# A table's loads pinned in the load queue, and their wait for sixteen writes

## The chip, the core and the metric

The kernel runs on one core of a Trainium2 chip. The core has five engines that follow their own in-order queues: PE (TensorE, matrix products), DVE (VectorE), ACT (ScalarE), POOL (GpSimd) and SP (SyncE, which here issues loads). The metric is the device time of one execution in microseconds (us); lower is better. Runs of this kernel agree within about 0.06%, so that a difference of 0.2% can be told from none.

## What is computed

Two transformer blocks follow one another on 256 tokens of width 2048. The change touches only the last part of the second block, a layer of 16,384 small experts. Its reference, cut down:

```
q = (hb @ w_query).reshape(PEER_BLOCK, PEER_HEADS, 2, D_KEY // 2)
s = einsum('thpc,hpnc->thpn', q, sub_keys)      # scores against 2 x 128 keys, 8 heads
...                                             # top 16 pairs per head and token: idx, best_s
g = softmax(best_s)
u_sel = take(u, idx);  a = gelu(einsum('thkd,td->thk', u_sel, hb))
v_sel = take(v, idx)
out = einsum('thk,thkd->td', g * a, v_sel)
```

The kernel gathers no rows of `u` and `v`. It computes the activations of all 16,384 experts for all tokens (the first product, with `u`), multiplies them by a table of gates that is zero wherever a token did not choose an expert, and multiplies the result by all of `v` (the second product). The table lies in the chip's memory: `gd`, one value for each pair of expert and token.

## The kernel before

**The first product** is driven in `experts_in` by `linear`, over 128 column tiles `c` of 128 experts. Its weights `in_pu` come in 256 loads of 512 KB (`half`, line 289, tile `raw`, four buffers). Each is split in two parts by ACT (line 276, `whi`, a rounded copy) and DVE (line 261, `wlo`, the rest), in two pieces of 128x512 each, so that three matrix products in fast format (`ph`·`whi`, `pl`·`whi`, `ph`·`wlo`, into the accumulator `plin`) give the accuracy of one in full format. `expert` ends each column tile: DVE scales the accumulator into `et` (line 261), ACT applies GELU and writes it to `A` (line 273).

**The table** is filled beside the first product. `choose` (DVE) finds experts `EI` and gates `GT`; `scatter` then has POOL issue 256 indirect writes with accumulation (line 1660), 128 for each half of the tokens, one slot for 128 tokens at a time. Sixteen writes belong to one head, so there are sixteen groups of sixteen. Two pairs of one head are never equal, but pairs of different heads can be, so each group waits until all sixteen writes before it have landed.

**The second product** is `experts_out`. For each of 128 steps `j` a tile `g` of the table (128x256, 128 KB) is loaded by SP (line 1766), POOL multiplies it by `A` (line 258), and ACT and DVE split the product into `wh` and `wl` (lines 276 and 261). Two weight loads of `in_pv` follow, split the same way, and 24 matrix products per load into eight accumulators `o`. At the end DVE adds the residual `res`, and the result is stored.

**The order of the work.** A scheduler sets each engine's order when the program is built, from a simulated timeline of its own. Code under `tc.high_priority()` may be moved ahead of code that stands before it: the weight loads and splits in `half`, and the load, product and split of `g` in `experts_out`. An engine runs its queue strictly in that order, so an instruction that waits holds up all that is queued behind it. `keep_in_program_order` takes an instruction out of that freedom; `add_manual_dep` adds an edge: `Sync` makes a wait, `NoSync` only an order on one engine.

Of the kernel before, what the change touches and what calls it, by code (L numbers as in the profile page):

```python
# [8 lines left out]
F32 = mybir.dt.float32  # L9
# [8 lines left out]
S = 256  # L18
# [226 lines left out]
class Kernel:  # L245
# [1339 lines left out]
    def experts_in(self):  # L1585

        nc = self.nc
        es = ExitStack()
        sp = self.sp = self.pool("sp", 1, es)
        ap = self.pool("ap", 1, es)  # L1590
        rf = self.rf
        self.iota = self.ones
        nc.sync.dma_start(self.iota, self.io["iota"])

        self.EI = [sp.tile([128, 128], U32, name=f"EI{b}") for b in range(2)]
        self.GT = [sp.tile([128, 128], F32, name=f"GT{b}") for b in range(2)]
        t = sp.tile([128, 128], F32, name="dg")
        self.tokc = sp.tile([128, 2], F32, name="tokc")
        self.vtt(t, self.ident, self.iota, OP.mult)
        nc.vector.tensor_reduce(self.tokc[:, 0:1], t, axis=AX.X, op=OP.add)  # L1600
        self.ts(self.tokc[:, 1:2], self.tokc[:, 0:1], 128.0, None, OP.add)
        self.chosen = set()

        def slot(name):
            return ap.tile([128, 32, S], F32, name=name, tag="A", bufs=4)

        s1, s2, s3 = (slot(n).rearrange("p c t -> p (c t)") for n in ("s1", "s2", "s3"))
        qx = s1[:, 0:4096].rearrange("p (c t) -> p c t", t=S)
        scv = s1[:, 4096:8192].rearrange("p (b c n) -> p b c n", b=2, n=NKEY)
        keys = s2[:, 0:2048].rearrange("p (c n) -> p c n", n=NKEY)  # L1610
        nc.sync.dma_start(keys, self.io["keys"])
        pq = {}

        def query(c, p):
            self.vtt(qx[:, c], p, rf, OP.mult)
            if c % 4 == 0:
                pq[0], pq[1] = self.ps("psc"), self.ps("psc")
            for tb in range(2):
                self.mm(pq[tb][:, 128 * (c % 4):128 * (c % 4) + 128], qx[:, c, 128 * tb:128 * tb + 128], keys[:, c])
                if c % 4 == 3:  # L1620
                    self.acp(scv[:, tb, c - 3:c + 1], pq[tb].rearrange("p (c n) -> p c n", c=4))

        self.lin(self.io["w_pq"], 0, KT, KT, self.pxh, self.pxl, S, query)
        A = self.A = {}

        def expert(c, p):
            k, i = divmod(c, 32)
            if k not in A:
                A[k] = slot(f"A{k}")
            t = sp.tile([128, S], F32, name="et", tag="et", bufs=3)  # L1630
            self.vtt(t, p, rf, OP.mult)
            self.act(A[k][:, i], t, AF.Gelu)

        self.drive(self.linear(self.io["pu"], 0, NKEY, KT, self.pxh, self.pxl, S, expert),
                   [[self.both(self.choose(0, scv[:, 0], s2[:, 2048:4096], s2[:, 4096:8192]),
                               self.choose(1, scv[:, 1], s3[:, 2048:4096], s3[:, 4096:8192]))],
                    [self.scatter()]], EVERY3, (1,))
        self.rstack.close()
        return es
# [110 lines left out]
    def experts_out(self, es):  # L1750
        nc, A, sp = self.nc, self.A, self.sp
        with ExitStack() as c:
            vp = self.pool("vp", 2, c)
            op = self.pool("op", 1, c)
            acc = self.pool("acc", 1, c, space=PSUM)

            P = [[None] * 4 for _ in range(2)]
            for d in (3, 2, 0, 1):
                for b in range(2):
                    P[b][d] = acc.tile([128, 512], F32, name=f"o{b}{d}")  # L1760
            table = self.gd.rearrange("(i j t) o -> i j (t o)", j=NKEY, t=S)
            for j in range(NKEY):
                w = A[j // 32][:, j % 32]
                with self.tc.high_priority():
                    g = sp.tile([128, S], F32, name="g", tag="g", bufs=2)
                    nc.sync.dma_start(g, table[:, j])
                    self.gtt(g, w, g, OP.mult)
                    wh, wl = ((sp if j == 0 else vp).tile([128, S], F32R, name=n) for n in ("wh", "wl"))
                    self.split(wh, wl, g)
                for hf in range(2):  # L1770
                    hi, lo = self.half(self.io["pv"][2 * j + hf])
                    first, last = j == 0, j == NKEY - 1
                    for d in range(2):
                        for b in range(2):
                            ts = slice(128 * b, 128 * b + 128)
                            for l, r, st, en in ((wh, hi, first, False), (wh, lo, False, False), (wl, hi, False, last)):
                                self.mm(P[b][2 * hf + d], l[:, ts], self.block(r, 4 * d, 4), st, en)
            res = op.tile([128, 2, D], F32, name="res")
            nc.sync.dma_start(res, self.hd.rearrange("b p d -> p b d"))
            for b in range(2):  # L1780
                for d in range(4):
                    r = res[:, b, 512 * d:512 * d + 512]
                    self.vtt(r, P[b][d], r, OP.add)
                    nc.sync.dma_start(self.out[128 * b:128 * b + 128, 512 * d:512 * d + 512], r)
        es.close()
# [20 lines left out]
```

## Time and profile before

| | us |
|---|---|
| median of three runs | 3704.99 |
| the three runs | 3704.28 to 3706.61 |
| the profiled execution | 3704.27 |
| its span in the trace | 3702.5 |

The trace divides the span into busy time of each engine. PE is busy for 93% of it and bounds the kernel in almost every stage. The exception is one stretch, two slices of 40 long, in which PE, DVE and ACT are all idle and only POOL works. The span leaves out 1.77 us of the profiled execution's time.

### The profile page before, as it was taken

The numbers are of one execution on the slowest core, as the hardware profiler recorded it, in microseconds if no ns is written. First come the engines' busy times: TensorE is split into PE (matmuls) and PEld (weight loads), VectorE is DVE, ScalarE is ACT, GpSimd is POOL, SyncE is SP. The second block draws the span as 40 slices with busy tenths as digits, with TensorE's granted clock in tenths as the row PEclk, the third lists the DMA queues.
The fourth block names the chain that finished last, engine by engine and source line by source line (L and its number), as shares of the span: only waits on it lengthen the run. The fifth ranks groups of instructions, "written<-read, shape, count | busy, mean of one in ns | idle before, by whom it ended". The sixth has DMA issues, their size and how long they took to land.

```text
span 3702.5 us, 72372 instructions
## 1 busy us (share of the span) xinstructions
PE 3449.7 (93%) x28376; PEld 3238.5 (87%) x28376; DVE 2289.7 (62%) x4248; ACT 1764.2 (48%) x3187; POOL 869.4 (23%) x788
## 2 busy tenths in 40 slices
PE   8999999999999999999999999996019999999999
PEld 7899899999999999999999999996019988888887
DVE  6677777755555576565675998553005556666565
ACT  5444555545454554444554555552005555555554
POOL 2222221300000043000120006777760011111111
PEclk9999999999999999999999999998559999999999
DMA  5334545667676755443466567775225577666666
GB/s 196 110 111 136 162 145 155 202 196 218 196 221 194 221 189 164 143 148 120 132 188 195 184 187 186 186 188 103 0 32 185 187 226 211 212 211 212 212 211 195
DMA packets 230279, 635.99 MB, mean 172 GB/s; under 512 B 58320, under 2 KB 75408, under 8 KB 229552
## 3 DMA queue, kind: packets, MB, share of 16 engines
q1 hardware_dynamic: 193072, 631.22, 54.8%
q0 software_dynamic: 36864, 0.15, 2.5%
q8 instruction: 222, 3.64, 0.4%
q14 instruction: 121, 0.99, 0.1%
HBM read 610.16 MB, written 21.10 MB: 170 GB/s over the span
## 4 chain that ended last, share of the span: by engine, by line
PE 89%; POOL 5%; DVE 2%; issue 2%; DMA 2%; ACT 0%; SPq 0%; DVEq 0%; POOLq 0%; ACTq 0%
PE plin L255 63%; PE o L255 19%; POOL gd L1660 5%; DMA gd<-GT,EI 1%; PE po L255 1%; DVE wlo L261 1%; PE pfz L255 1%; PE pw L255 0%; DMA hd<-ht 0%; PE pz L255 0%; PE pbc L255 0%; PE pix L255 0%; PE pcs L255 0%; PE px L751 0%; PE pt L751 0%
## 5 line engine op out<-in xcount | busy, mean ns | idle before, releaser
L261 DVE TENSOR_TENSOR wlo<-raw,whi 128x512 fp32r<-128x512 f32 x2208 | 1615.4, 733 | 974.6 <-ACT whi L276 919.2
L276 ACT ACTIVATE whi<-raw 128x512 fp32r<-128x512 f32 x2208 | 1389.2, 630 | 1438.6 <-PE plin L255 1004.5
L255 PE MATMUL plin<-ph,whi 128*128 128x256 f32 (+1 forms) x4560 | 1285.7, 282 | 212.1 <-ACT whi L276 210.5
L255 PE MATMUL plin<-ph,wlo 128*128 128x256 f32 (+1 forms) x4560 | 1290.4, 283 | 2.2 <-DVE wlo L261 2.2
L255 PE MATMUL plin<-pl,whi 128*128 128x256 f32 (+1 forms) x4560 | 1290.4, 283 | 0.0
L255 PEld LDWEIGHTS plin<-ph,whi 128*128 128x128 f32 x4560 | 863.1, 189 | 213.8 <-ACT whi L276 210.7
L255 PEld LDWEIGHTS plin<-ph,wlo 128*128 128x128 f32 x4560 | 863.4, 189 | 4.7 <-DVE wlo L261 2.6
L255 PEld LDWEIGHTS plin<-pl,whi 128*128 128x128 f32 x4560 | 858.2, 188 | 1.6 <-issue 1.1
L1660 POOL DMA_INDIRECT gd<-GT,EI x256 | 407.1, 1590 | 415.4 <-DVE wlo L261 296.6
L255 PE MATMUL o<-whi,wl 128*128 128x512 f32 x1024 | 405.5, 396 | 0.0
L255 PE MATMUL o<-wlo,wh 128*128 128x512 f32 x1024 | 404.5, 395 | 0.0
L255 PE MATMUL plin<-xh,whi 128*128 128x256 f32 x1136 | 329.3, 290 | 9.1 <-ACT whi L276 8.1
L255 PE MATMUL plin<-xh,wlo 128*128 128x256 f32 x1136 | 328.9, 290 | 4.1 <-DVE wlo L261 3.9
L255 PE MATMUL plin<-xl,whi 128*128 128x256 f32 x1136 | 328.2, 289 | 1.5 <-DVE xl L264 1.5
L255 PE MATMUL o<-whi,wh 128*128 128x512 f32 x1024 | 321.9, 396 | 0.6 <-ACT whi L276 0.6
L258 POOL TENSOR_TENSOR g<-A,g 128x256 f32<-128x256 f32 x128 | 103.3, 808 | 816.2 <-DMA g<-gd 786.5
L255 PE MATMUL plin<-uh,wlo 128*128 128x256 f32 x1024 | 289.7, 283 | 0.0
L255 PE MATMUL plin<-ul,whi 128*128 128x256 f32 x1024 | 289.7, 283 | 0.0
L255 PE MATMUL plin<-uh,whi 128*128 128x256 f32 x1024 | 289.6, 283 | 0.0
L255 PEld LDWEIGHTS o<-whi,wh 128*128 128x128 f32 x1024 | 192.3, 188 | 47.3 <-issue 0.7
L255 PEld LDWEIGHTS o<-whi,wl 128*128 128x128 f32 x1024 | 192.2, 188 | 47.3
L255 PEld LDWEIGHTS plin<-xh,whi 128*128 128x128 f32 x1136 | 220.9, 195 | 13.8 <-ACT whi L276 9.4
(563 smaller groups left out, 3462.8 us busy)
## 6 DMA issues: line engine op xcount, KB each, us to landing
raw<-in_pu_dram SPq DMA_DIRECT2D x256, 512.0 KB, 3.7
raw<-in_pv_dram SPq DMA_DIRECT2D x256, 512.0 KB, 4.3
raw<-in_w_in_dram SPq DMA_DIRECT2D x208, 512.0 KB, 3.5
raw<-in_w_up_dram SPq DMA_DIRECT2D x128, 512.0 KB, 4.5
raw<-in_w_down_dram SPq DMA_DIRECT2D x128, 512.0 KB, 4.1
raw<-in_w_mix_dram SPq DMA_DIRECT2D x32, 512.0 KB, 3.6
gd<-zero SPq DMA_DIRECT2D x64, 256.0 KB, 5.2
raw<-in_w_out_dram SPq DMA_DIRECT2D x32, 512.0 KB, 3.6
```

The lines of the kernel that those rows point to most:

```text
L255: self.nc.tensor.matmul(out, l, r, start=start, stop=stop)
L258: self.nc.gpsimd.tensor_tensor(out, a, b, op=op)
L261: return self.nc.vector.tensor_tensor(out, a, b, op=op)
L276: return self.nc.scalar.activation(out, a, AF.Copy, **kw)
L1660: i = self.nc.gpsimd.indirect_dma_start(self.gd, bass.IndirectOffsetOnAxis(self.EI[tb][:, s:s + 1], 0), self.GT[tb][:, s:s + 1], None, com ...
```

## The change

Three lines change in kind. The ring of `et` goes from three buffers to two; the ring of `g` goes from two to three. Every load of `g` is kept in program order, so that it stands in SP's queue behind the loads that the code issues before it, all of `in_pu` among them. The first load of `g` gets a wait for each of the last sixteen writes (`self.scattered`), and every later one an order edge to the one before it.

```
-            t = sp.tile([128, S], F32, name="et", tag="et", bufs=3)
+            t = sp.tile([128, S], F32, name="et", tag="et", bufs=2)
...
+            sync, order = (mybir.DependencyInfo(c, mybir.DependencyReason.DATA)
+                           for c in (mybir.DependencyClass.Sync, mybir.DependencyClass.NoSync))
+            prev = None
             for j in range(NKEY):
                 w = A[j // 32][:, j % 32]
                 with self.tc.high_priority():
-                    g = sp.tile([128, S], F32, name="g", tag="g", bufs=2)
-                    nc.sync.dma_start(g, table[:, j])
+                    g = sp.tile([128, S], F32, name="g", tag="g", bufs=3)
+                    i = self.tc.keep_in_program_order(nc.sync.dma_start(g, table[:, j]))
+
+                    for x in [prev] if prev else self.scattered:
+                        self.tc.add_manual_dep(i.ins, x.ins.name, order if prev else sync, reason="the table is complete")
+                    prev = i
```

SP's queue before, where the first load of the table stands (`raw` is a weight load, `g` a tile of the table; the numbers are buffers):

```order
L289 DMA raw_33783<-in_pu_dram 128x1024
L289 DMA raw_33818<-in_pu_dram 128x1024
L1766 DMA g_36607<-gd_9608 128x256
L1766 DMA g_36658<-gd_9608 128x256
L289 DMA raw_33857<-in_pu_dram 128x1024
L1766 DMA g_36709<-gd_9608 128x256
L289 DMA raw_33892<-in_pu_dram 128x1024
```

And SP's queue with the change, at the place where these loads now stand:

```order
L289 DMA raw_36614<-in_pv_dram 128x1024
L289 DMA raw_36636<-in_pv_dram 128x1024
L289 DMA raw_36665<-in_pv_dram 128x1024
L289 DMA raw_36687<-in_pv_dram 128x1024
L289 DMA raw_36716<-in_pv_dram 128x1024
L1769 DMA g_36607<-gd_9608 128x256
L1769 DMA g_36658<-gd_9608 128x256
L1769 DMA g_36709<-gd_9608 128x256
L289 DMA raw_36738<-in_pv_dram 128x1024
L1786 DMA res_43135<-hd_25560 128x2x2048
```

The three first table loads have moved past the rest of the first product's weights and past five loads of the second's.

ACT's queue before, around the split of the table's first tile, `wh_36610` (`whi` are parts of weights, `A2` a column tile of activations):

```order
L276 ACTIVATE whi_33711<-raw_33709 128x512
L276 ACTIVATE whi_33715<-raw_33709 128x512
L276 ACTIVATE whi_33746<-raw_33744 128x512
L276 ACTIVATE wh_36610<-g_36607 128x256
L276 ACTIVATE whi_33750<-raw_33744 128x512
L273 ACTIVATE A2_31854<-et_33705 128x256
L276 ACTIVATE whi_33785<-raw_33783 128x512
```

ACT's queue with the change, around the same split:

```order
L273 ACTIVATE A3_34223<-et_36444 128x256
L276 ACTIVATE whi_36616<-raw_36614 128x512
L276 ACTIVATE whi_36620<-raw_36614 128x512
L276 ACTIVATE whi_36638<-raw_36636 128x512
L276 ACTIVATE whi_36642<-raw_36636 128x512
L273 ACTIVATE A3_34223<-et_36518 128x256
L276 ACTIVATE wh_36610<-g_36607 128x256
L276 ACTIVATE wh_36661<-g_36658 128x256
L276 ACTIVATE wh_36712<-g_36709 128x256
L276 ACTIVATE whi_36667<-raw_36665 128x512
```

The split has moved from among the first product's weights to behind its last GELU (`et_36518`) and behind the splits of the second product's first two weight loads. DVE's half of the split moves with it.

## Rows read from the trace of the kernel before

**Rows 1.** The page: span, engines' busy time, and busy tenths in 40 slices.
```profile
span 3702.5 us, 72372 instructions
...
PE 3449.7 (93%) x28376; PEld 3238.5 (87%) x28376; DVE 2289.7 (62%) x4248; ACT 1764.2 (48%) x3187; POOL 869.4 (23%) x788
...
PE   8999999999999999999999999996019999999999
...
POOL 2222221300000043000120006777760011111111
PEclk9999999999999999999999999998559999999999
```
**Rows 2.** Waits, 2540 to 2800 us: who waited for whom, us, times, longest.
```profile
ACT wh L276 <- POOL g L258: 214.3, 1, 214.3
...
PE plin L255 <- ACT whi L276: 210.5, 1, 210.5
...
POOL gd L1660 <- DMA gd<-GT,EI: 17.2, 7, 4.2
```
**Rows 3.** Timeline: start, duration, engine, line, operation, [idle before].
```profile
2759.66 1.54 POOL L1660 DMA_INDIRECT gd<-GT,EI  x1 [0.30 <-issue]
2762.64 0.80 SPq L1766 DMA_DIRECT2D g<-gd  x2
...
2764.92 1.40 POOL L258 TENSOR_TENSOR g<-A,g 128x256 f32<-128x256 f32 x2 [3.72 <-DMA g<-gd]
2765.68 0.42 ACT L276 ACTIVATE wh<-g 128x256 fp32r<-128x256 f32 x1 [214.34 <-POOL g L258]
```
**Rows 4.** Timeline of PE at both ends of the wait and between the products.
```profile
2555.85 0.28 PE L255 MATMUL plin<-ph,wlo 128*128 128x256 f32 x1
2766.66 0.58 PE L255 MATMUL plin<-ph,whi 128*128 128x256 f32 x1 [210.54 <-ACT whi L276]
...
2980.01 0.28 PE L255 MATMUL plin<-ph,wlo 128*128 128x256 f32 x1
...
2980.85 0.48 PE L255 MATMUL o<-whi,wh 128*128 128x512 f32 x1 [0.56 <-ACT whi L276]
```
**Rows 5.** Windows: length, busy us of PE, PEld, DVE, ACT, POOL, PE clock, DMA.
```profile
2232.00:2556.00 324.00, 324.00 (x2740) 323.92 (x2738) 207.24 (x365) 166.03 (x285) 244.69 (x151) 1.00 0.76 184
2556.00:2558.00 2.00, 0.12 (x2) 0.00 (x0) 0.00 (x0) 0.00 (x0) 1.70 (x2) 1.00 0.21 0
2558.00:2560.00 2.00, 0.00 (x0) 0.00 (x0) 0.00 (x0) 0.00 (x0) 1.64 (x2) 0.67 0.21 0
2560.00:2766.00 206.00, 0.00 (x0) 0.00 (x0) 0.00 (x0) 0.33 (x2) 159.78 (x105) 0.50 0.21 3
2766.66:2770.00 3.34, 3.33 (x14) 3.11 (x15) 2.64 (x5) 2.10 (x5) 1.17 (x1) 0.50 0.61 162
2770.00:2771.00 1.00, 1.00 (x9) 1.00 (x9) 0.97 (x2) 0.77 (x2) 0.00 (x0) 0.84 0.99 320
...
3000.00:3690.00 690.00, 690.00 (x2958) 555.46 (x2958) 422.60 (x616) 349.60 (x616) 98.45 (x122) 1.00 0.69 210
```
**Rows 6.** Timeline of POOL: the first writes of five groups of sixteen.
```profile
2265.85 1.92 POOL L1660 DMA_INDIRECT gd<-GT,EI  x1 [2.96 <-DMA gd<-GT,EI]
...
2305.10 1.54 POOL L1660 DMA_INDIRECT gd<-GT,EI  x1 [5.01 <-DMA gd<-GT,EI]
...
2339.59 2.02 POOL L1660 DMA_INDIRECT gd<-GT,EI  x1 [4.71 <-DMA gd<-GT,EI]
...
2543.59 1.54 POOL L1660 DMA_INDIRECT gd<-GT,EI  x1 [4.23 <-DMA gd<-GT,EI]
...
2731.98 1.55 POOL L1660 DMA_INDIRECT gd<-GT,EI  x1 [2.20 <-DMA gd<-GT,EI]
```
**Rows 7.** POOL's writes in two stretches, 2339 to 2543.5 and 2543.5 to 2762.
```profile
L1660 POOL DMA_INDIRECT gd<-GT,EI x96 | 152.9, 1593 | 51.5 <-issue 27.8 <-DMA gd<-GT,EI 20.1 <-DVE wlo L261 3.7
L1660 POOL DMA_INDIRECT gd<-GT,EI x112 | 172.6, 1541 | 49.2 <-issue 32.0 <-DMA gd<-GT,EI 17.2
```
**Rows 8.** Line 1660's own view: its 256 writes, issue to landing.
```profile
DMA to landing us min/median/max: 2.8/3.5/6.1
```
**Rows 9.** SP's timeline near the second product's start, and the page's load sizes.
```profile
2967.45 11.69 SPq L289 DMA_DIRECT2D raw<-in_pv_dram  x5
...
raw<-in_pv_dram SPq DMA_DIRECT2D x256, 512.0 KB, 4.3
```
**Rows 10.** Tiles `et` and `A`, 2494 to 2503 us: first and last start.
```profile
L261 DVE TENSOR_TENSOR et<-plin,rf x2: 424/424/424, 2495.1 to 2500.8; 128x256 f32<-128x256 f32 x2
L273 ACT ACTIVATE A<-et x2: 419/420/420, 2495.6 to 2501.2; 128x256 f32<-128x256 f32 x2
```
**Rows 11.** Waits in the second product, 3000 to 3690 us.
```profile
POOL g L258 <- DMA g<-gd: 557.1, 117, 6.6
...
ACT wh L276 <- PE o L255: 66.1, 111, 0.6
...
ACT wh L276 <- POOL g L258: 7.1, 12, 0.6
```

## The prediction, made before the changed kernel was run

> **What bounds the kernel now.** I read the page first. PE is busy for 93% of the span, and the slices show where it is not: it is at nine tenths or more from the second slice on, but falls to 6, 0 and 1 tenths in slices 28 to 30, where POOL alone is busy and the granted clock falls too [rows 1]. So I asked next who waits for whom there. PE waits once, 210.5 us, for ACT's split of a weight; ACT's longest wait, 214.3 us, is that of `wh`, the split of the table's first tile, for POOL's product `g` [rows 2]. The weights are not late. ACT's queue holds the table's split in front of the next weight's split, and an in-order queue makes the weight wait for the table.
>
> The timeline shows what ends it. The last indirect write is issued at 2759.66, the first load of the table goes out at 2762.64, POOL multiplies at 2764.92 and ACT splits at 2765.68 [rows 3]. PE starts again at 2766.66 and has 213.6 us of the first product left, up to 2980.01 + 0.28 = 2980.29 [rows 4]. So a job of some 210 us that PE could do lies behind a table that it does not need for that job.
>
> **What the change removes.** In the new order of ACT the table's split stands behind the last weight split and the last GELU of the first product, and in SP's queue the table's first load stands behind all first-product weights and five loads of the second's. Nothing of the first product then waits for the writes. PE stops at 2555.85 + 0.28 = 2556.13 today [rows 4]; with the change it goes on. What is left is 2980.29 - 2766.66 = 213.63 us, less what the restart costs: the clock stands at 0.50 (1.2 GHz) from 2766.66 to 2770.00 and for some 0.32 us of the next one (0.84 = 1 - 0.5 x 0.32) [rows 5], so 3.66 us at half speed, which loses 1.83 us. First product's end: 2556.13 + 213.63 - 1.83 = 2767.9.
>
> **When the table is ready.** Today's writes run undisturbed during the wait; with the change they run beside PE, ACT, DVE and weight loads. A group of sixteen took (2543.59 - 2339.59) / 6 = 34.00 us while the first product ran and (2731.98 - 2543.59) / 6 = 31.40 us in the wait [rows 6]. Six of the groups that ran in the wait will now run beside the first product, so I take 34.0 for the six from 2543.59: the seventh starts at 2747.6 instead of 2731.98. Today that one takes 2762.64 - 2731.98 = 30.66 us up to the table's load, 2.98 of them behind the last write [rows 3, 6]. With the change about 20 us of it still lie beside the first product, where a write comes every 1.593 + 0.30 = 1.89 us, and the rest where it comes every 1.84 [rows 3, 7]; with fifteen steps that is 28.2, and 2.98 make 31.2. Table load: 2778.8. (If all of it ran at the disturbed rate, 34.0 - 0.7 = 33.3, it would be 2780.9.)
>
> The new wait is for sixteen writes where the old one was for the last alone. The other fifteen are older; the slowest landing seen is 6.1 us [rows 8], and the last but one was issued 1.85 us earlier, so this adds between nothing and 6.1 - 1.85 - 2.98 = 1.3 us. I take nothing, since the median landing of 3.5 us [rows 8] ends earlier than the last write's.
>
> From the load's issue to the end of `wh` today: 2765.68 + 0.42 - 2762.64 = 3.46 us [rows 3]. Three table loads now go together, but the first does not wait for the others. So the second product starts at 2778.8 + 3.5 = 2782.3, and PE stands still for 2782.3 - 2767.9 = 14.4 us, where it now waits 0.56 us at this place [rows 4].
>
> **What waits behind the new wait.** SP stands at the first table load from about 2767 to 2778.8. Behind it are two more table loads, the sixth weight load of the second product and `res`. Five weight loads are ahead, enough for two and a half steps, that is 14 us of PE at 5.6 us a step (3702.5 - 2980.85 = 721.65 us for 128 steps [rows 1, 4]). A weight load lands 4.3 us after its issue [rows 9], so I cost this at nothing; without that cover it would be one landing, 4.3 us, once. ACT and DVE have split the first two weight loads before they reach `wh`, which is why PE needs `wh` alone.
>
> **The other edits.** `et` with two buffers: DVE writes one every 5.7 us and ACT has read it 0.9 us after DVE's start [rows 10], so even one buffer would do: nothing. `g` with three buffers lets a table load go earlier: in the second product 111 of the waits of `wh` are for PE, which frees its buffer, and only 12, together 7.1 us, for POOL [rows 11]. There the table is early already; PE is busy 690.00 of 690 us [rows 5], and earlier loads give nothing. The order edges add no instruction.
>
> **The clock.** In today's wait the clock is full for the two microseconds after PE's stop, 0.67 in the next two, 0.50 from 2560 on [rows 5]. A gap of 14.4 us is long enough for the same, so the second product pays the 1.83 us that the first no longer pays. From its start to the span's end today: 3702.5 - 2980.85 = 721.65 us; with the restart 723.5.
>
> **Sum.** 2782.3 + 723.5 = 3505.8 us of span, 196.7 less than 3702.5: 210.5 of wait go, 13.8 of wait come, the restart moves. The execution lies 1.77 us above its span (3704.27 against 3702.5), and the median of the runs 0.72 above that execution: 3508.3, **3508 us**.
>
> **A page against a term.** The disturbed group is 2.6 us longer, and the rows divide this: the writes themselves are 16 x (1593 - 1541) ns = 0.8 us longer, and the waits between groups are (20.1 + 3.7) / 6 = 4.0 against 17.2 / 7 = 2.5 us [rows 7]. The Trainium skill, "SBUF — State Buffer", section "Who interferes with whom", says that a VectorE subtraction of two SBUF tensors, as `wlo` is, takes only the read side of the port pair shared with GpSimd, and infers that descriptor writing is not held up by it. By that rule alone the writes would keep 31.4 us a group in their new surroundings. The rows show a small loss where the rule has none, and the larger part in the landings, of which it says nothing here; I keep 34.0, and the rule's result is the first rival.
>
> **Rivals.**
> Undisturbed writes: seven groups at 31.4 us put the last landing at 2762.6, before the first product's end. Then the table's load is held by its place in SP's queue: the fifth weight load before it is issued by 2979.14 today, 1.15 us before the first product's end [rows 4, 9], so at 2766.8 with the change. 2766.8 + 0.3 + 3.5 = 2770.6, a gap of 2.7 us; with 721.65 and up to 1.83 for the clock the span is 3492 to 3494, the time 3496 with the same 2.5 added. For it speaks the low busy share of the new last group; against it six groups in a row at 34.0.
>
> More disturbed writes: one group, from 2265.85 to 2305.10, took 39.25 us [rows 6], while DVE still chose experts. Nothing of that kind runs in the new stretch. Were all seven like it, the load would go at 2543.59 + 274.8 - 0.7 = 2817.6, and the time would be 2817.6 + 3.5 + 723.5 + 2.5 = 3547.
>
> Slower than before: each table load now keeps its place between the weight loads, which wait for buffers. If `wh` became late by this, every step of the second product would wait. The gain is 196.7 us and there are 127 later steps, so it decides from 1.55 us a step; at 2 us the time is 3508 + 254 = 3762. Against it: the third buffer lets a load go earlier, not later, the new order repeats the old one (two weight loads, one table load), and `wh` is early in 111 of 123 waits [rows 11].
>
> The wait stays: if a weight of the first product were still queued behind the table on SP, ACT or DVE, PE would wait until 2766 as now, and the time would be 3705. The printed orders speak against it.
>
> **Chances and range.** My forecast 0.82, with a range of its own of 3503 to 3516 (a quicker last group or a slower landing, the 1.3 us of the sixteen writes, a first step that is not smooth); undisturbed writes 0.07; more disturbed 0.08; slower 0.02; the wait stays 0.01. The range takes in the forecast and the undisturbed case, and reaches some way towards the third: 3495 to 3522. What can be told from no change is 0.2%, 7 us: faster 0.97, same 0.01, slower 0.02.
>
> **What would show it.** In the new profile the three slices of PE at 6, 0 and 1 are gone but for one short dip. PE's longest wait stands between the last `plin` and the first `o`, 12 to 17 us, and it is for ACT's `wh`, not for `whi`. POOL's groups stay near 34 us up to about 2768. The clock shows one short stay at 0.50 around 2780. `et` makes nobody wait. I would be wrong if the groups lengthen beyond 36 us, if the first product itself runs slower beside the writes than today's 324.00 / 2740 = 0.118 us a product [rows 5], or if waits for POOL's `g` repeat in every step.

## The result, and the profile after

The changed kernel takes 3507.5 us (median of four runs, 3504.2 to 3508.8) where the kernel before takes 3705.8 in the same comparison. The ratio is 0.946, with an interval from 0.945 to 0.948: 198 us faster. The prediction was 3508.

The page of the changed kernel answers [rows 1]: the span, the busy time of each engine, and three of the lines of forty slices.

```profile
span 3507.0 us, 72378 instructions
PE 3448.0 (98%) x28376; PEld 3237.5 (92%) x28376; DVE 2298.0 (66%) x4248; ACT 1764.2 (50%) x3187; POOL 877.2 (25%) x788
...
PE   8999999999999999999999999999999899999999
...
POOL 2222213310101015200012000477777611111111
PEclk9999999999999999999999999999999999999999
```

The three slices in which PE was nearly idle have become one slice at 8. POOL's work has not become shorter: it now stands in slices in which PE is busy. The waits (engine, line and tile that waited, what for: total, times, longest) answer [rows 2], the first line over the whole span, the two others from 2540 to 2800:

```profile
PE o L255 <- ACT wh L276: 15.8, 1, 15.8
...
ACT wh L276 <- POOL g L258: 15.2, 3, 14.4
POOL gd L1660 <- DMA gd<-GT,EI: 28.4, 7, 5.2
```

The one long wait of PE, 210.5 us inside the first product, is gone. In its place stands one of 15.8 us between the products, again for ACT's `wh`, and ACT again waits for POOL's `g`. The timeline shows the new chain, the answer to [rows 3, 4] (start, duration, engine, line, operation, and in brackets the idle time before it and what ended it):

```profile
2755.36 11.69 SPq L289 DMA_DIRECT2D raw<-in_pv_dram  x5
...
2767.92 0.28 PE L255 MATMUL plin<-ph,wlo 128*128 128x256 f32 x1
...
2777.64 1.54 POOL L1660 DMA_INDIRECT gd<-GT,EI  x1 [0.30 <-issue]
...
2780.64 1.28 SPq L1769 DMA_DIRECT2D g<-gd  x3
...
2782.80 2.27 POOL L258 TENSOR_TENSOR g<-A,g 128x256 f32<-128x256 f32 x3 [3.63 <-DMA g<-gd]
...
2783.55 0.42 ACT L276 ACTIVATE wh<-g 128x256 fp32r<-128x256 f32 x1 [14.45 <-POOL g L258]
...
2784.02 0.80 PE L255 MATMUL o<-whi,wh 128*128 128x512 f32 x1 [15.83 <-ACT wh L276]
```

The first product ends at 2768.2, the last write is issued at 2777.64, and the table's load goes 3.00 us behind it. PE starts again at 2784.02. So the table is still what PE waits for, but only over the 15.8 us by which its chain outlasts the first product.

The starts of the first and of the seventh group of writes from there on, to be held against [rows 6]:

```profile
2544.15 1.54 POOL L1660 DMA_INDIRECT gd<-GT,EI  x1 [4.29 <-DMA gd<-GT,EI]
...
2749.30 1.77 POOL L1660 DMA_INDIRECT gd<-GT,EI  x1 [3.92 <-DMA gd<-GT,EI]
```

Six groups took (2749.30 - 2544.15) / 6 = 34.19 us each, as the disturbed ones before did (34.0), and not 31.4. The seventh took 2780.64 - 2749.30 = 31.34 us from its start to the load; 18.9 us of that, up to 2768.2, still lay beside the first product.

The windows around the new gap answer [rows 5] (from and to, length, PE busy with its count, granted clock, where 1.00 is 2.4 GHz and 0.50 is 1.2 GHz, DMA share, GB/s):

```profile
2768.20:2770.00 1.80, 0.00 (x0) 1.00 0.71 228
2770.00:2772.00 2.00, 0.00 (x0) 1.00 0.23 8
2772.00:2774.00 2.00, 0.00 (x0) 0.82 0.19 0
2774.00:2780.00 6.00, 0.00 (x0) 0.50 0.25 0
2780.00:2784.00 4.00, 0.00 (x0) 0.50 0.54 146
2784.00:2787.00 3.00, 2.98 (x7) 0.51 0.96 382
2787.00:2788.00 1.00, 1.00 (x5) 1.00 1.07 434
```

The clock falls in the gap, and PE works its first 3 us of the second product at 1.2 GHz. That costs it about half of 2.98 us, 1.5 us, in place of the 1.83 us that the first product paid before.

### The profile page after: what moved, and what is told of

It reads as the page before. It is cut to its first block, busy times and chain, and to the rows that moved or that the text cites. A ratio compares the mean times of both kernels' runs of the same rounds, so it can differ in the third digit from the quotient of the medians.

```text
span 3507.0 us, 72378 instructions
## 1 busy us (share of the span) xinstructions
PE 3448.0 (98%) x28376; PEld 3237.5 (92%) x28376; DVE 2298.0 (66%) x4248; ACT 1764.2 (50%) x3187; POOL 877.2 (25%) x788
## 4 chain that ended last, share of the span: by engine, by line
PE 87%; POOL 6%; DVE 2%; DMA 2%; issue 2%; ACT 1%; DVEq 0%; POOLq 0%; SPq 0%; ACTq 0%
PE plin L255 60%; PE o L255 20%; POOL gd L1660 5%; DMA gd<-GT,EI 1%; DVE wlo L261 1%; PE po L255 1%; PE pfz L255 1%; DMA hd<-ht 0%; PE pw L255 0%; PE pbc L255 0%; PE pz L255 0%; PE pix L255 0%; PE pcs L255 0%; DVE xl L264 0%; PE pt L751 0%
## 5 line engine op out<-in xcount | busy, mean ns | idle before, releaser
L261 DVE TENSOR_TENSOR wlo<-raw,whi 128x512 fp32r<-128x512 f32 x2208 | 1597.8, 725 | 954.6 <-ACT whi L276 905.4
L255 PE MATMUL o<-whi,wh 128*128 128x512 f32 x1024 | 324.1, 397 | 15.8 <-ACT wh L276 15.8
L255 PEld LDWEIGHTS o<-wlo,wh 128*128 128x128 f32 x1024 | 192.8, 188 | 47.3
```

The lines of the kernel that those rows point to most:

```text
L255: self.nc.tensor.matmul(out, l, r, start=start, stop=stop)
L261: return self.nc.vector.tensor_tensor(out, a, b, op=op)
```

## Experiments

Unless it is said otherwise, an edit stands against the changed kernel. The kernel before ran again beside them: 3705.5 us beside the pin alone, the rings alone, the late split and the earlier start; 3706.7 beside the freed load, the load in front and the two that leave something out; 3703.7 beside the later start and the two repeats. Beside the first four it ran 21 times, from 3700.8 to 3711.5 us, a spread of 0.3% and not the 0.06% of its first three runs, so that a difference of some 0.1% between two medians means little here.

**Which edit does it.** The pin and its waits alone, with the old rings, and the rings alone, without the pin:

```
-            t = sp.tile([128, S], F32, name="et", tag="et", bufs=2)
+            t = sp.tile([128, S], F32, name="et", tag="et", bufs=3)
...
-                    g = sp.tile([128, S], F32, name="g", tag="g", bufs=3)
+                    g = sp.tile([128, S], F32, name="g", tag="g", bufs=2)
```

> The pinned loads and their sixteen waits alone; both rings keep the sizes of the kernel before (et 3, g 2). Order theory (the whole gain is the place of the table's first load and split in the queues): 3507 to 3510 us, ratio 0.946 to 0.948, PE's longest wait 14 to 17 us between the products. Rival (the third buffer of g carries part of it, since each later table load is freed earlier): at 1 us a step the time would be 3507 + 127 = 3634, with waits for POOL's g in every step.

```
-                    i = self.tc.keep_in_program_order(nc.sync.dma_start(g, table[:, j]))
-
-                    for x in [prev] if prev else self.scattered:
...
+                    nc.sync.dma_start(g, table[:, j])
```

> The two rings alone (et 2, g 3), nothing pinned and no new wait. Order theory: the table's first split stays among the first product's weights (in the built order it still stands behind 89 of 128 GELUs), so PE waits about 210 us and the time is that of before, 3702 to 3708. Rival (the rings carry the gain): well under 3700.

The pin alone took 3507.9 us (0.9465, 0.9450 to 0.9479), all of the change's gain; PE's wait in its trace is 17.8 us, a little above the 14 to 17 that I expected, in the slowest of its four executions (3515.5 us). The rings alone took 3705.8 (1.0003, 0.9994 to 1.0013), with PE's wait at 210.2 us as before. The two rings are worth nothing here.

**Which queue held PE.** The pin moves two things at once: the load in SP's queue, by its own words, and, because the scheduler follows, the split in ACT's queue. Each can be left early while the other is late. First, the kernel before with only the first split kept in program order, so that ACT does it after all of the first product's, while the load stays early in SP's queue:

```
-                    self.split(wh, wl, g)
+                    if j == 0:
+                        self.tc.keep_in_program_order(self.acp(wh, g))
+                        self.tc.keep_in_program_order(self.vtt(wl, g, wh.bitcast(F32), OP.subtract))
+                    else:
+                        self.split(wh, wl, g)
```

> The kernel before with one edit: ACT's and DVE's split of the table's first tile stand behind the first product, as after the change, but the table's first load keeps its early place in SP's queue, with 72 weight loads of the first product behind it. Theory A (ACT's place of the split alone made the 210 us): PE runs on and the time is that of the change, 3507 to 3512. Theory B (SP's place of the load holds PE as well, and is only hidden behind ACT's): PE eats the weights that are loaded, about three halves at 2.84 us, and stops at about 2565 until the first weight load behind the table lands, 2763.5 + 3.8 = 2767 and its split, 2768.5; a wait of about 204 us instead of 210.5, time 3697 to 3704.

It took 3701.9 us (0.9990, 0.9981 to 0.9999). The waits of PE (whole span), of ACT and of SP's queue (2540 to 2800), and SP's timeline:

```profile
PE plin L255 <- ACT whi L276: 215.8, 2, 207.5
...
ACT whi L276 <- DMA raw<-in_pu_dram: 212.3, 2, 211.6
...
SPq L1766 <- DMA gd<-GT,EI: 217.5, 1, 217.5
...
2499.86 51.44 SPq L289 DMA_DIRECT2D raw<-in_pu_dram  x19
2768.84 0.80 SPq L1766 DMA_DIRECT2D g<-gd  x2
2769.74 20.15 SPq L289 DMA_DIRECT2D raw<-in_pu_dram  x10
```

SP stands for 217.5 us at the table's load, and the remaining weights of the first product are not even asked for until 2769.74. ACT now waits for such a weight and no longer for the table. PE runs some 10 us further than before, on the weights already loaded, and then waits 207.5 us.

The other way round: the first three table loads go out from POOL's queue, behind the writes, and SP is free of them; ACT's split stays early.

```
-                    nc.sync.dma_start(g, table[:, j])
+                    (nc.gpsimd if j < 3 else nc.sync).dma_start(g, table[:, j])
```

> The mirror of the run with the late split: the kernel before, with the first three table loads issued by POOL behind its own writes, so that nothing of the table stands in SP's queue before the second product, while ACT's split of the table's first tile keeps its early place (behind 89 of 128 GELUs). Theory (each of the two places is enough alone to hold PE): PE waits some 210 us for ACT and the time is 3702 to 3709. Rival (SP's queue is what holds, ACT's place only follows it): the gain of the change, 3507 to 3520.

It took 3704.6 us (1.0000, 0.9990 to 1.0009). Its waits of ACT, PE and SP's queue, from 2540 to 2800:

```profile
ACT wh L276 <- POOL g L258: 212.3, 1, 212.3
PE plin L255 <- ACT whi L276: 208.5, 1, 208.5
SPq L289 <- DVE wlo L261: 252.0, 17, 213.8
```

Now SP waits only for a weight buffer to come free: it has loaded ahead as far as it can, and the weights are there. ACT holds PE instead, at `wh`. So there were two locks on the same door. Each alone holds PE for some 208 us, and an edit that opens one of them is worth next to nothing: 3.6 us in the first case, no difference in the second. In both runs PE's wait is for the same tile, `whi`; only the waits of SP and ACT tell which queue it was. The kernel before had both waits: beside ACT's 214.3 us [rows 2], its trace shows this one of SP's queue (2540 to 3702):

```profile
SPq L1766 <- DMA gd<-GT,EI: 214.8, 1, 214.8
```

**Whether what is left is the end of the writes.** `EVERY3` says after how many steps of the first product one step of the work beside it, choosing experts and then writing, is issued. With 7 the writes start earlier, with 9 later:

```
-EVERY1, EVERY2, EVERY3 = (6, 6, 7), 8, 8
+EVERY1, EVERY2, EVERY3 = (6, 6, 7), 8, 7
```

> The changed kernel with the expert choice and the writes stepped every 7 blocks of the first product instead of 8. The first write stands behind some 67 steps of 2.84 us, so it should go out 67 x 2.84 / 8 = 24 us earlier, and so should the last. Theory (the 15.8 us that PE still waits are the end of the writes and nothing else): the writes end at about 2757, before the first product, and the table's load is held only by its place behind the fifth weight load, about 2767; PE's wait falls to 2.5 to 3 us, span 3491.5 to 3494, ratio about 0.9425. Rival (the denser choice on DVE costs PE as much as it gives back, or the wait has another cause): 3500 us or more.

> The changed kernel with the choice and the writes stepped every 9 blocks instead of 8: the writes start and end some 20 to 24 us later (every 7 blocks made them start 20.6 us earlier). Theory (the end of the writes sets the second product's start, one for one): PE's wait between the products grows from 15.8 to 36 to 40 us and the time from 3508 to 3528 to 3532. Rival (writes that start later run faster, or something else ends PE's wait): less than 3520.

With 9 the time was 3533.3 us (0.9543, 0.9529 to 0.9558), a little above the 3528 to 3532 that I expected. PE's wait and SP's first table load:

```profile
PE o L255 <- ACT wh L276: 38.1, 1, 38.1
...
2801.29 1.28 SPq L1769 DMA_DIRECT2D g<-gd  x3
```

The load comes 20.65 us later than in the changed kernel, the first product ends 1.5 us earlier, and the wait is 38.1 - 15.8 = 22.3 us longer: what the writes lose, PE loses. With 7 the time was 3499.6 us (0.9442, 0.9429 to 0.9455), and the wait did not vanish:

```profile
PE o L255 <- ACT wh L276: 3.9, 1, 3.9
...
2757.44 11.69 SPq L289 DMA_DIRECT2D raw<-in_pv_dram  x5
2769.43 1.27 SPq L1769 DMA_DIRECT2D g<-gd  x3
```

The first write went out 20.6 us earlier, but the wait fell by 11.9 us only. The last write is issued at 2753.45, 16 us before the load, and the load now goes directly behind the five weight loads of the second product: its place in SP's queue, not the writes, sets it. I had expected a span of 3491.5 to 3494 and got 3498.2. Of the difference, about 1 us is a wait of 3.9 where I expected 2.5 to 3, 1.0 lies in the second product, and 2.1 us in stages long before the writes, where this execution was slower and nothing had been changed.

**A version that is faster than the change.** If SP's queue sets it, the load must stand in front of those five. Pinning the first step's two weight loads as well puts them behind the table's load in program order:

```
+EVERY1, EVERY2, EVERY3 = (6, 6, 7), 8, 7
...
-                    hi, lo = self.half(self.io["pv"][2 * j + hf])
+                    hi, lo = self.half(self.io["pv"][2 * j + hf], j == 0)
```

> The changed kernel with the choice and the writes stepped every 7 blocks, and the second product's first two weight loads kept in program order too, so that the table's first load stands directly behind the first product's weights instead of behind five loads of the second's. With the writes' end at 2755 and the table's load there, ACT's queue runs: last GELU, table's split, first weight split. PE's wait is then DVE's scaling (0.4), the GELU (0.4), the table's split (0.4) and the weight's split (0.6), about 2.1 us instead of 3.9, short enough that the clock may stay at full: 2 to 4 us less than the run that starts earlier, 3496 to 3498, ratio 0.943 to 0.944. Rival (order within a few us does not matter, or SP now waits for the writes and weight loads come late): 3499 us or more.

It took 3494.6 us (0.9433, 0.9421 to 0.9446), below the 3496 to 3498 that I expected. Its SP queue, PE's wait between the products, and the windows around it (columns as above):

```profile
2755.92 0.33 SPq L1769 DMA_DIRECT2D g<-gd  x1
2756.34 1.74 SPq L289 DMA_DIRECT2D raw<-in_pv_dram  x2
...
PE o L255 <- ACT whi L276: 1.8, 1, 1.8
...
2767.80:2769.60 1.80, 0.01 (x1) 1.00 0.37 59
2769.60:2771.00 1.40, 1.40 (x6) 1.00 0.60 222
2771.00:2772.00 1.00, 1.00 (x4) 0.50 1.08 459
2772.00:2773.80 1.80, 1.80 (x5) 0.50 0.98 414
2773.80:2775.00 1.20, 1.20 (x5) 0.74 0.99 420
```

The load leaves 13.5 us earlier than with the earlier writes alone, and PE now waits 1.8 us, for a weight. The gap went from 15.8 to 1.8 and the span from 3507.0 to 3492.8, both by 14 us. The change and this version then ran beside each other on one chip:

> The changed kernel unaltered, beside the next one on one chip: 3507 to 3509 us.

> The run with the earlier start and the table's load directly behind the first product's weights, beside the changed kernel on one chip. PE's wait between the products was 1.8 us there and 15.8 with the change, so it should be 14 us faster: 3493 to 3495.

The change took 3509.0 us (0.9472, 0.9459 to 0.9485) with a wait of 16.0 us, this version 3496.5 (0.9438, 0.9425 to 0.9451) with one of 1.8 us. The runs do not overlap: 3504.6 to 3512.4 against 3494.1 to 3498.5. It is 12.5 us faster than the change, where I had expected 14. The two profiled spans, 3507.2 and 3496.6, differ by 10.6 only, although the wait is 14.2 us shorter: this version's first load of `in_pu` went out at 2030.1 and the change's at 2026.0, so that 4.1 us were lost before the first product.

The version with the earlier writes alone did not run on that chip. Its 3499.6 us stand against 3494.6 and 3496.5, with intervals of the ratio that overlap; that the place of the load adds to the earlier writes rests on PE's wait in the traces, 1.8 us against 3.9.

**Why a group of writes is longer beside the first product.** Two candidates work beside it: the weight loads, and DVE's subtraction. Each was left out alone, from the middle of the first product on. Such a kernel no longer computes the layer, and each ran once (3496.9 us without the loads, 3499.2 without the subtraction); only the writes are read from them.

```
+            late = self.mode is not None and self.seen >= 128
...
+            if late and self.mode == "loads":
+                raw = self.kept
...
+                if late and self.mode == "split":
+                    h = l = self.phi.tile([128, QB, 128], F32R, name="whi", tag="whi")
+                    i = self.acp(h, r)
```

> The changed kernel without the second half of the first product's weight loads: from the 129th on, the weights of the 128th stay in their buffer and are split and multiplied again (all else as before, so the last 64 column tiles are those of other experts). The question is what makes a group of sixteen writes 34.1 us beside the first product and 31.4 in the old wait. Theory L (the landings wait behind weight loads): groups from about 2441 us on take 31.4 + 0.8 = 32.2 us, waits between groups near 2.5 us, single writes still 1.59 us in the mean; the table's load goes some 10 x 1.8 = 18 us earlier. Theory P (DVE's subtractions hold up the writing of descriptors): groups stay near 34.

> The changed kernel without DVE's subtraction in the second half of the first product: from the 129th weight load on, the rounded part stands in for the rest too (wlo is left out, all loads and matrix products remain). Theory L (landings behind weight loads make most of the 2.7 us): groups take 34.1 - 0.8 = 33.3 us, single writes 1.54 us, waits between groups stay near 4 us. Theory P: groups fall to 31.4.

The groups of line and operation for the writes between 2441 and 2745: the count, the total and the mean in ns of one, and the idle time before them. In this order: the changed kernel, without the loads, without the subtraction; then, in the same order, the time from issue to landing (least, median, most).

```profile
L1660 POOL DMA_INDIRECT gd<-GT,EI x144 | 230.2, 1599 | 77.6 <-issue 40.9 <-DMA gd<-GT,EI 32.7 <-DVE wlo L261 4.0
L1677 POOL DMA_INDIRECT gd<-GT,EI x152 | 242.3, 1594 | 64.4 <-issue 44.1 <-DMA gd<-GT,EI 18.2 <-DVE wlo L261 2.1
L1677 POOL DMA_INDIRECT gd<-GT,EI x150 | 231.1, 1541 | 76.8 <-issue 41.4 <-DMA gd<-GT,EI 35.3
...
DMA to landing us min/median/max: 3.0/4.7/5.9
DMA to landing us min/median/max: 2.8/3.0/4.3
DMA to landing us min/median/max: 3.9/4.7/5.9
```

Over nine groups the pitch is (2749.30 - 2441.81) / 9 = 34.17 us in the changed kernel, (2729.20 - 2437.60) / 9 = 32.40 without the loads and (2734.85 - 2440.16) / 9 = 32.74 without the subtraction. The loads cost 1.8 us a group, and they do it by the landing, whose median goes from 4.7 to 3.0 us while the write itself stays at 1594 ns. The subtraction costs 1.4, and 16 x (1599 - 1541) ns = 0.9 of it lies in the writes themselves, while the median landing stays at 4.7. The other 0.5 us lies in POOL's waits between the groups, in the mean 3.97 us in the changed kernel, 3.46 without the subtraction and 2.25 without the loads. Without the subtraction these waits run from 2.1 to 4.7 us; why is not shown. Together the two costs are 3.2, somewhat more than the 2.8 that separate 34.2 from the 31.4 of the old wait. Perhaps they overlap a little; no run leaves out both.

How the subtraction does this can be seen write by write. POOL and DVE of the changed kernel, from 2545 to 2556:

```profile
2545.99 2.01 POOL L1660 DMA_INDIRECT gd<-GT,EI  x1 [0.30 <-issue]
2548.30 1.54 POOL L1660 DMA_INDIRECT gd<-GT,EI  x1 [0.30 <-issue]
2551.99 1.98 POOL L1660 DMA_INDIRECT gd<-GT,EI  x1 [0.30 <-issue]
...
2545.89 0.69 DVE L261 TENSOR_TENSOR wlo<-raw,whi 128x512 fp32r<-128x512 f32 x1 [0.72 <-ACT whi L276]
2548.73 0.69 DVE L261 TENSOR_TENSOR wlo<-raw,whi 128x512 fp32r<-128x512 f32 x1 [0.77 <-ACT whi L276]
2551.86 0.69 DVE L261 TENSOR_TENSOR wlo<-raw,whi 128x512 fp32r<-128x512 f32 x1 [0.99 <-ACT whi L276]
```

The first and the third write begin while a subtraction runs, and are 0.47 and 0.44 us longer than the second, which begins between two subtractions. The subtractions beside them end 0.59 and 0.56 us after the write's start. So it is all along: of 151 writes from 2441 to 2761, 53 begin well inside a subtraction, and each is longer by what is left of that subtraction less 0.11 to 0.13 us; 29 begin within 0.04 us of its start and are not longer, while 27 of their subtractions take 0.72 to 0.76 us in place of 0.69; and the 69 others take 1.54 to 1.56 us.

## Why the prediction was right

The steps, with what each measured:

| step | predicted | measured |
|---|---|---|
| end of the first product | 2767.9 | 2768.2 |
| pitch of a group beside it | 34.0 | 34.19 |
| start of the seventh group | 2747.6 | 2749.30 |
| from there to the table's load | 31.2 | 31.34 |
| cost of waiting for sixteen writes | 0 | 0.02 |
| load to the end of `wh` | 3.46 | 3.33 |
| PE's wait | 14.4 | 15.83 |
| second product | 723.5 | 722.98 |
| span | 3505.8 | 3507.0 |

**The gain** is the wait of 210.5 us gone and 15.8 us put in its place, as the sum had it: by the spans -195.5 us against -196.7. The job behind the wait was still the same length, and the restart of the clock moved from the first product to the second.

**The new wait was undersized by 1.4 us.** The step is the start of the seventh group, 1.7 us late: 0.56 us because the first of the six began at 2544.15 and not 2543.59, and 6 x 0.19 = 1.1 because each was that much longer. The end of the first product, 0.3 us late, takes a little of it back.

**The waits for sixteen writes** cost what I took, nothing: the load leaves 3.00 us after the last write's issue, where it left 2.98 us after it before. What is queued behind the waiting load on SP was hidden as well: the sixth weight load of the second product leaves at once behind it, at 2782.0, and PE does not wait once in the second product from 2786 on.

**The clock** cost 1.5 us where I took 1.83; with it taken off, the second product is 721.5 us against today's 721.65.

**The median** agrees better than its parts. The span was 1.2 us longer than the sum, and the profiled execution lay 1.25 us above its median, where I had added 0.72 the other way. The half microsecond between 3508 and 3507.5 is two errors that cancel.

**Where the reasoning was thinner than the result.** I read the hold in ACT's queue, from [rows 2], and took from it that the weights are not late. SP's queue came in only as a place from which the load moves, and in the last rival, with a chance of 0.01. Yet the same trace has SP's wait of 214.8 us for the table, with the remaining weights of the first product behind it, and the runs show that either queue was enough alone. Here the pin moved both, so the time came out; for a change that had moved the split alone, the same reading would have promised some 200 us, and the run of that took 3702.

**The disturbance of the writes** I split as 0.8 us in the writes and 1.5 in the landings. The runs agree on the landings, 1.8 us, and show the cause, the weight loads. For the writes the Trainium skill, "SBUF — State Buffer", section "Who interferes with whom", infers that such a subtraction does not hold up descriptor writing. The trace shows that it holds up the write instruction, by up to 0.47 us here; whether in the descriptors or in reading `GT` and `EI` from SBUF, no run separates. The same section says that a VectorE instruction with two SBUF inputs contends with a GpSimd instruction that reads SBUF, and with that the rows agree. Keeping 34.0 was right. The rival of undisturbed writes, 3496, did not come, nor did the more disturbed 3547: from 2544 on no group was longer than 35.1 us. The first product did not run slower beside the writes either: 536.20 / 4532 = 0.118 us a product from 2232 to 2768.2.

## What to carry to other kernels

When one engine waits, look at every in-order queue in front of it, not only at the one that the wait names: two queues can hold the same work, and freeing one of them shows nothing. A load that depends on a long side job belongs in its queue behind everything that does not need it, but ahead of what is wanted after it: the change won the first 198 us, and the place in front of five loads, with writes that start 20 us earlier, 12.5 more. What is then left between two stages is the end of the side job against the end of the main one, and the price of running both together (here 34.2 us a group against 31.4) belongs in that sum.

## What the runs showed of the hardware that I had not expected

An indirect write (1.54 us) that begins inside a DVE subtraction of two tiles in SBUF is longer by what is left of the subtraction less some 0.12 us (53 of 53); where one begins with it, the subtraction is longer instead, mostly by 0.03 to 0.04 us. The landing of such a write takes 4.7 us in the median beside weight loads and 3.0 without them.

The granted clock can fall after the gap that PE left is over. In the version with the load in front, PE stood still for 1.8 us, worked 1.4 us at full clock, and only then, at 2771.0, did the clock fall to 0.50, for 1.0 + 1.8 us and about half of the next 1.2. In its repeat, after a gap of 1.79 us, the clock fell within 0.1 us of PE's start: 0.54 from 2773.40 to 2774.60. I had expected that so short a gap might leave it at full.
